# Hybrid decoder trunk: token-major residual, and the down projections as seven products of half matrices with weight sums made by accumulating DMAs

## The chip, the cores and the metric

One NeuronCore of a Trainium2 chip runs the whole program as one launch. The metric is device time in microseconds, the median of the runs; lower is better. TensorE (PE in the profile; PEld is its weight load) multiplies out of SBUF into PSUM, VectorE (DVE) and ScalarE (ACT) do element-wise work, GpSimd (POOL) does small work and issues the DMAs that add, and SyncE (SP) issues the plain DMAs.

## The reference, cut to what matters

Two layers work on x of 512 tokens by 1024 channels in float32; D_FF is 2816.

```python
def swiglu(h, w1, w3, w2):
    return (jax.nn.silu(h @ w1) * (h @ w3)) @ w2
...
    for l in range(DEPTH):
        h = rmsnorm(x, ffn1_norm[l])
        x = x + FFN_RESIDUAL * swiglu(h, ffn1_w1[l], ffn1_w3[l], ffn1_w2[l])
        h = rmsnorm(x, mix_norm[l])
        p = h @ w_in[l]
...
        mix = jnp.concatenate([y_a, y_b, y_c, y_d], axis=-1)
        x = x + mix @ w_out[l]
        h = rmsnorm(x, ffn2_norm[l])
        x = x + FFN_RESIDUAL * swiglu(h, ffn2_w1[l], ffn2_w3[l], ffn2_w2[l])
    return rmsnorm(x, final_norm)
```

The four mixers y_a to y_d (a convolution of 31 taps with a layer norm, a short gated convolution, a pooling and a gating by 128x128 matrices) are the same in both kernels.

## The kernel before, in words

**Products.** Every float32 operand is split into two float32r parts, hi (a ScalarE cast, L92) and lo (a VectorE subtract, L94), and every product is three matmuls (mm3, L97 to L100): hi by hi, hi by lo, lo by hi. PSUM tiles have 512 columns. TensorE takes its work in the order in which the program is written (a manual schedule); the other engines' orders come from the scheduler, and each engine runs its own list in order.

**Residual.** x is held with channels on partitions, as eight tiles x0 to x7 of 128 channels by 512 tokens. The norm is split off: Norm.gained (L144) multiplies a tile by the channel gain while splitting it, which needs no statistic, and the factor 1/rms of each token is applied behind the products. Its statistic comes from squares summed over tiles (L153), four narrow matmuls (rstd_of, L116), a power on GpSimd (L112) and four transposes (spread, L128), all while TensorE is at work on the next stage.

**One feed-forward block** (ffn, L172). For each of 22 tiles of 128 channels of D_FF the up part runs 2 x 8 mm3 of 512 columns, weights stationary and tokens moving, and makes the tile a with sigmoid and three VectorE multiplications (up, L177). The down part (L242) runs for each of 8 channel tiles m of the output 22 mm3, 528 matmuls in all; the sum is scaled by half the norm's factor and added to x[m] (L237), and the next norm takes the tile at once (nxt.add). Four such blocks, f0a, f0b, f1a and f1b, and a mixer stage (mixers, L303) between each layer's two. In the mixers two more pieces matter here: the gating values are products with tokens on the output partitions, 256 columns wide (L362 to L364), and the conformer's 62 taps (L502) run on VectorE beside TensorE's other work.

**Weights.** load_w (L88) loads a tile of up to 128x1024 on SP's queue into one of four raw buffers and splits it into one of four hi and lo pairs, so loads run ahead by as much as these buffers allow. All buffers are named slots: a DMA into a slot waits until the last reader of the earlier tile in it is done.

**Start and end.** Ten matmuls on a constant (WARM) stand first, then the first tile's matmuls follow the loads of x tile by tile (L191 to L216). At the end the last channel tile runs in two halves of the tokens, and class Last (L273) takes each half through the final norm and out.

## Time and profile before

| | |
|---|---|
| median of 3 runs | 1746.85 us (1746.84 to 1747.02) |
| span of the profiled execution | 1744.5 us, 2.35 us under that median |
| PE busy | 1733.9 us, 99% of the span |
| PEld busy | 1438.9 us, 82% |
| DVE busy | 877.9 us, 50% |
| ACT busy | 533.5 us, 31% |
| POOL busy | 22.0 us, 1% |
| DMA | 170.70 MB, mean 98 GB/s |

PE's busy time counts a matmul from its start to its modelled end, and these overlap; the pace is read from the distance between the starts of two matmuls. The profiled execution shows its span, from the first to the last instruction, and the runs give the time of whole executions; a sum made against the span is carried to the runs by their difference.

### The profile page before, as it was taken

How to read it: one execution, taken by the hardware profiler on the slowest of the kernel's cores; microseconds unless marked ns; L12 is line 12 of the kernel's file. 1: busy time of each engine (PE TensorE's matmuls, PEld its weight loads, DVE VectorE, ACT ScalarE, POOL GpSimd, SP SyncE). 2: the span in 40 equal slices, each digit the busy share in tenths (PEclk: the TensorE clock that was granted, in tenths of full speed). 3: DMA queues.
4: the chain of work that ended last, by engine and by line, in shares of the span. 5: the costliest groups of instructions: out<-in, count | busy, mean ns of one | idle time of the engine just before them, and what ended most of it. 6: DMA issues, size and time to landing. Idle time of an engine off the chain costs nothing.

```text
span 1744.5 us, 19177 instructions
## 1 busy us (share of the span) xinstructions
PE 1733.9 (99%) x7882; PEld 1438.9 (82%) x7882; DVE 877.9 (50%) x1145; ACT 533.5 (31%) x693; POOL 22.0 (1%) x22
## 2 busy tenths in 40 slices
PE   9999999999999999999999999999999999999997
PEld 7888888888788888888888888888888888888887
DVE  6444443459864444434344444433697554444333
ACT  5222222233243222222232222222333432222221
POOL 0000000000000000000000000000000000000000
PEclk9999999999999999999999999999999999999999
DMA  5222223332232222333322322233222322223321
GB/s 208 97 97 97 97 88 100 103 115 79 85 103 97 97 97 97 94 95 93 105 97 97 97 97 94 91 100 117 89 85 91 103 97 97 97 97 91 97 91 48
DMA packets 52022, 170.70 MB, mean 98 GB/s; under 512 B 5728, under 2 KB 8928, under 8 KB 51936
## 3 DMA queue, kind: packets, MB, share of 16 engines
q1 hardware_dynamic: 51936, 169.50, 30.0%
q8 instruction: 61, 1.00, 0.2%
q14 instruction: 25, 0.20, 0.0%
HBM read 167.38 MB, written 2.10 MB: 97 GB/s over the span
## 4 chain that ended last, share of the span: by engine, by line
PE 99%; DVE 0%; ACT 0%; DMA 0%; issue 0%; SPq 0%; POOLq 0%; DVEq 0%; ACTq 0%
PE p_f1b L98 7%; PE p_f1b L100 7%; PE p_f1a L98 7%; PE p_f1b L99 7%; PE p_f0b L100 7%; PE p_f0b L99 7%; PE p_f0b L98 7%; PE p_f1a L100 7%; PE p_f1a L99 7%; PE p_f0a L100 7%; PE p_f0a L98 7%; PE p_f0a L99 7%; PE pi_L L98 3%; PE pi_L L99 3%; PE pi_L L100 3%; PE po_L L98 2%
## 5 line engine op out<-in xcount | busy, mean ns | idle before, releaser
L502 DVE SCALAR_TENSOR_TENSOR cg_L<-cv_L,pt,cg_L 128x503 f32<-128x503 f32 (+26 forms) x120 | 83.5, 726 | 2.3 <-ACT cg_L L500 1.8
L98 PE MATMUL p_f1b<-gh_b,whi_f1bb 128*128 128x512 f32 x176 | 68.6, 390 | 0.0
L98 PE MATMUL p_f1a<-gh_a,whi_f1ab 128*128 128x512 f32 x176 | 68.6, 390 | 0.0
L98 PE MATMUL p_f0b<-gh_b,whi_f0bb 128*128 128x512 f32 x176 | 68.6, 390 | 0.0
L98 PE MATMUL p_f0b<-gh_b,whi_f0ba 128*128 128x512 f32 x176 | 68.6, 390 | 0.0
L98 PE MATMUL p_f1a<-gh_a,whi_f1aa 128*128 128x512 f32 x176 | 68.6, 390 | 0.0
L98 PE MATMUL p_f1b<-gh_b,whi_f1ba 128*128 128x512 f32 x176 | 68.6, 390 | 0.0
L100 PE MATMUL p_f0b<-gh_b,wlo_f0bb 128*128 128x512 f32 x176 | 68.5, 389 | 0.0
L100 PE MATMUL p_f1b<-gh_b,wlo_f1bb 128*128 128x512 f32 x176 | 68.5, 389 | 0.0
L100 PE MATMUL p_f0b<-gh_b,wlo_f0ba 128*128 128x512 f32 x176 | 68.5, 389 | 0.0
L100 PE MATMUL p_f1a<-gh_a,wlo_f1ab 128*128 128x512 f32 x176 | 68.5, 389 | 0.0
L100 PE MATMUL p_f1b<-gh_b,wlo_f1ba 128*128 128x512 f32 x176 | 68.5, 389 | 0.0
L99 PE MATMUL p_f1a<-gl_a,whi_f1aa 128*128 128x512 f32 x176 | 68.5, 389 | 0.0
L100 PE MATMUL p_f1a<-gh_a,wlo_f1aa 128*128 128x512 f32 x176 | 68.5, 389 | 0.0
L99 PE MATMUL p_f0b<-gl_b,whi_f0ba 128*128 128x512 f32 x176 | 68.5, 389 | 0.0
L99 PE MATMUL p_f1b<-gl_b,whi_f1ba 128*128 128x512 f32 x176 | 68.5, 389 | 0.0
L99 PE MATMUL p_f1a<-gl_a,whi_f1ab 128*128 128x512 f32 x176 | 68.5, 389 | 0.0
L99 PE MATMUL p_f0b<-gl_b,whi_f0bb 128*128 128x512 f32 x176 | 68.5, 389 | 0.0
L99 PE MATMUL p_f1b<-gl_b,whi_f1bb 128*128 128x512 f32 x176 | 68.5, 389 | 0.0
L98 PE MATMUL p_f0a<-gh_n,whi_f0ab 128*128 128x512 f32 x168 | 65.5, 390 | 0.0
L98 PE MATMUL p_f0a<-gh_n,whi_f0aa 128*128 128x512 f32 x168 | 65.5, 390 | 0.0
L99 PE MATMUL p_f0a<-gl_n,whi_f0aa 128*128 128x512 f32 x168 | 65.4, 389 | 0.0
(1074 smaller groups left out, 4434.7 us busy)
## 6 DMA issues: line engine op xcount, KB each, us to landing
raw_f0ba<-w SPq DMA_DIRECT2D x22, 512.0 KB, 3.7
raw_f0bb<-w SPq DMA_DIRECT2D x22, 512.0 KB, 3.6
raw_f1aa<-w SPq DMA_DIRECT2D x22, 512.0 KB, 3.7
raw_f1ab<-w SPq DMA_DIRECT2D x22, 512.0 KB, 3.6
raw_f1ba<-w SPq DMA_DIRECT2D x22, 512.0 KB, 3.7
raw_f1bb<-w SPq DMA_DIRECT2D x22, 512.0 KB, 3.6
raw_f0aa<-w SPq DMA_DIRECT2D x21, 512.0 KB, 3.7
raw_f0ab<-w SPq DMA_DIRECT2D x21, 512.0 KB, 3.6
```

What stands on the lines that cost most here:

```text
L98: PE.matmul(ps, hi, xh, start=first, stop=False)
L99: PE.matmul(ps, hi, xl, start=False, stop=False)
L100: PE.matmul(ps, lo, xh, start=False, stop=last)
L502: V.scalar_tensor_tensor(acc[:, kk:], v[:, : T - kk], cw, acc[:, kk:], ALU.mult, ALU.add)
```

## The change

The residual and the norms become token-major. x is four tiles x0 to x3 of 128 tokens by 1024 channels. A norm is now whole ahead of the products: per token tile two squares with a sum along the row (Norm.square), the power on GpSimd and one multiplication by factor and gain over 1024 columns (Norm.scale), and then eight TensorE transposes, two casts and two subtracts (Norm.turn) that give the channel-major hi and lo tiles gh0, gh1, gl0 and gl1. Token tiles 2 and 3 come first, tiles 0 and 1 last. The first two tiles of an up part (heads), and the first gate and value in the mixers, therefore run in two halves of 256 columns with a turn of token tiles 0 and 1 between them. silu is one activation out of PSUM.

The down part multiplies the two halves of the tokens, of D_FF and of the output as 2x2 blocks, and takes seven products of halves in place of eight. A product (letters a to g in the names) has 11 channel tiles in six pieces j of two tiles (the last one) and, for each, 2 token tiles x 3 matmuls of 512 columns, activations stationary and weights moving: 66 matmuls, 462 for a block. Sums of activation quarters are made on VectorE (sums), sums of weight quarters by DMAs: gather loads one quarter on SP's queue and then adds another onto it with accum_op on GpSimd's queue. The running weight sum of products b, d and f lies in three tiles tt0, tt1 and tt2, which use the slots of gh0, gh1 and gl0. TensorE's order is a0 b0 a1 b1 to a5 b5, c0 d0 to c5 d5, e0 f0 to e5 f5, then g. Each product's sum is added to one to three places of x straight out of PSUM (add).

The rest: WARM is 40; the gains are loaded as 128x1024 tiles; the weights of w2 and w_out are laid out anew; the output projection has tokens on the output partitions.

```diff
+                S.activation(
+                    sq, xt[b][:, c * T : (c + 1) * T], AF.Square, scale=1.0 / 32.0,
+                    accum_out=self.ss[b][:, c : c + 1],
...
+        def scale(self, b):
...
+                y = rsqrt(v, 1, f"{self.name}{b}")
+                xn = tmp.tile([P, D], F32, tag="xn", name=f"xn_{self.name}{b}")
+                V.scalar_tensor_tensor(xn, xt[b], y, self.gain, ALU.mult, ALU.mult)
...
+        def turn(self, b):
+
+            with tc.high_priority(offset=400):
+                if self.hi is None:
+                    self.hi = [acts.tile([P, 4, T], F32R, tag=f"gh{q}", name=f"gh{q}_{self.name}") for q in range(2)]
+                    self.lo = [acts.tile([P, 4, T], F32R, tag=f"gl{q}", name=f"gl{q}_{self.name}") for q in range(2)]
+                s = slice(b * P, (b + 1) * P)
+                for q in range(2):
+                    ps = bank(f"pt_{self.name}{b}{q}", (P, 4, P))
+                    for k in range(4):
+                        c = (4 * q + k) * P
+                        PE.transpose(ps[:, k], self.xn[b][:, c : c + P], ident)
+                    S.copy(self.hi[q][:, :, s], ps)
+                    V.tensor_tensor(self.lo[q][:, :, s], ps, self.hi[q][:, :, s].bitcast(F32), ALU.subtract)
...
+        for r in (1, 0):
+            for _, _, _, _, ps, w in heads:
+                for e in range(2):
                     for k in range(KD):
                         c = slice(k * P, (k + 1) * P)
-                        mm3(p, w[0][:, c], w[1][:, c], nrm.h[k], nrm.l[k], k == 0, k == KD - 1)
-                    if j == j0 and p is p1:
-                        nrm.stats()
...
-        def down(m, p, c=slice(0, T)):
-            d = tmp.tile([P, T], F32, tag="h1", name=f"d_{name}{m}_{c.start}")
-            V.tensor_tensor(d[:, c], p, half[:, c], ALU.mult)
-            V.tensor_tensor(xt[m][:, c], xt[m][:, c], d[:, c], ALU.add)
-
-        for m in range(KD):
-            parts = ((0, 8), (8, 16), (16, KF))
-            ws = [load_w(w2[f, m, :, a * P : b * P], (b - a) * P, f"{name}c{m}_{a}") for a, b in parts]
...
-            p = psm.tile([P, T], F32, tag="mm", name=f"p2_{name}{m}")
-            for k in range(KF):
-                mm3(p, *weights(k), ah[k], al[k], k == 0, k == KF - 1)
-            down(m, p)
-            nxt.add(m)
...
+                        mm3(
+                            ps[e][:, HALF[r]], w[e][0][:, c], w[e][1][:, c],
+                            nrm.h(k)[:, HALF[r]], nrm.l(k)[:, HALF[r]], k == 0, k == KD - 1,
+                        )
+            if r == 1:
+                turns()
+        for h, j, i, k, ps, _ in heads:
+            out_of(ps[0], ps[1], h, j, i, k)
...
+        tt = [acts.tile([P, 4, T], F32, tag=("gh0", "gh1", "gl0")[q], name=f"tt{q}_{name}") for q in range(3)]
+
+        def tview(j):
+            n = SUB[j][1]
+            return tt[j // 2][:, (j % 2) * 2 : (j % 2) * 2 + n]
...
+        def gather(to, j, one, two):
+
+            k, n = SUB[j]
+            if one is not None:
+                nc.sync.dma_start(to, w2[f, one[0], one[1], :, k : k + n])
+            G.dma_start(to, w2[f, two[0], two[1], :, k : k + n], accum_op=ALU.add)
...
+        def product(banks, j, av, wv, more=False, tiles=(0, 1)):
+            n = SUB[j][1]
+            for t in tiles:
+                ts = slice(t * P, (t + 1) * P)
+                for i in range(n):
+                    mm3(
+                        banks[t], av[0][:, i, ts], av[1][:, i, ts], wv[0][:, i], wv[1][:, i],
+                        not more and j == 0 and i == 0, j == len(SUB) - 1 and i == n - 1, more,
                     )
...
+        def add(r, c, t, ps, sign):
+            b = 2 * r + t
+            xs = xt[b][:, c * T : (c + 1) * T]
+            with tc.high_priority(offset=400):
+                V.scalar_tensor_tensor(xs, ps, 0.5 * sign, xs, ALU.mult, ALU.add)
...
+        for j in J:
+            b11 = piece(0, 0, j, "a")
+            av, wv = asplit(quarter(0, 0, j), j, "a"), wsplit(b11, j, "a")
+            product(X, j, av, wv)
+            gather(tview(j), j, (0, 0), (0, 1))
+            av, wv = asplit(s1[j], j, "b"), wsplit(tview(j), j, "b")
+            product(Z, j, av, wv)
+        for t in range(2):
+            add(0, 0, t, X[t], 1)
+            add(1, 1, t, Z[t], 1)
+        Q = [bank(f"pq{t}_{name}") for t in range(2)]
+        for j in J:
+            t3 = wts.tile([P, SUB[j][1], T], F32, tag="raw", name=f"raw_{name}c{j}", bufs=4)
+            gather(t3, j, (0, 1), (1, 1))
+            av, wv = asplit(quarter(1, 0, j), j, "c"), wsplit(t3, j, "c")
+            product(Q, j, av, wv)
+            gather(tview(j), j, None, (1, 1))
+            av, wv = asplit(s2[j], j, "d"), wsplit(tview(j), j, "d")
+            product(X, j, av, wv, True)
+        for t in range(2):
+            add(1, 1, t, Q[t], -1)
+            add(0, 1, t, X[t], -1)
+            add(1, 0, t, X[t], 1)
+            add(1, 1, t, X[t], -1)
+            nxt.square(2 + t, 1)
+        W = [bank(f"pw{t}_{name}") for t in range(2)]
+        for j in J:
+            b21 = piece(1, 0, j, "e")
+            av, wv = asplit(quarter(0, 1, j), j, "e"), wsplit(b21, j, "e")
+            V.tensor_tensor(s2[j], s2[j], quarter(0, 1, j), ALU.add)
+            product(W, j, av, wv)
+            gather(tview(j), j, None, (1, 0))
+            av, wv = asplit(quarter(1, 1, j), j, "f"), wsplit(tview(j), j, "f")
+            product(Q, j, av, wv, True)
+        for t in range(2):
...
+        for t in range(2):
+            add(0, 0, t, W[t], 1)
+            nxt.square(t, 0)
+        held = []
+        for j in J:
+            b22 = piece(1, 1, j, "g")
+            av, wv = asplit(s2[j], j, "g"), wsplit(b22, j, "g")
+            if j < 4:
+                product(Z, j, av, wv, True)
+            else:
+                held.append((j, av, wv))
+            if j == 3 and not end:
+                for t in range(2):
+                    nxt.turn(2 + t)
+        for t in range(2):
+            for j, av, wv in held:
+                product(Z, j, av, wv, True, (t,))
+            add(0, 1, t, Z[t], 1)
+            nxt.square(t, 1)
+            if end:
+                nxt.last(t)
+            else:
+                nxt.scale(t)
```

The orders show where this puts the instructions. On SP's queue, around the start of f0a's down part, this stands before (raw_f0ac: the weights of the first two output tiles):

```order
L90 DMA raw_f0ab21_1730<-w13 128x1024
L90 DMA raw_f0ac0_0_1794<-w2 128x1024
L90 DMA raw_f0ac0_8_1800<-w2 128x1024
L90 DMA raw_f0ac0_16_1806<-w2 128x768
L90 DMA raw_f0ac1_0_1888<-w2 128x1024
```

and this stands there now (raw_f0aa2 to 4: product a; tt: the first quarter of product b's sums, in two calls each; raw_f0ac: product c):

```order
L91 DMA raw_f0aa2_1908<-w2 128x1024
L91 DMA raw_f0aa3_1952<-w2 128x1024
L91 DMA raw_f0aa4_1996<-w2 128x1024
L253 DMA tt2_f0a_1815<-w2 128x1024
L253 DMA tt0_f0a_1813<-w2 128x1024 x2
L253 DMA tt1_f0a_1814<-w2 128x1024 x2
L253 DMA tt2_f0a_1815<-w2 128x512
L91 DMA raw_f0aa5_2040<-w2 128x512
```

The loads into tt stand behind five loads of product a, and tt2 (piece 4) stands ahead of tt0 (pieces 0 and 1). On GpSimd's queue, which held nothing for a down part before, the adding DMAs now stand in the same order:

```order
L254 DMA tt2_f0a_1815<-w2 128x1024
L254 DMA tt0_f0a_1813<-w2 128x1024 x2
L254 DMA tt1_f0a_1814<-w2 128x1024 x2
L254 DMA tt2_f0a_1815<-w2 128x512
L254 DMA tt0_f0a_1813<-w2 128x1024 x2
```

The last of these rows is already product d's addition. On VectorE, between products d and e, f of f0a, eight additions to x (L281) now stand between the splits of e0 and of f0 (before, a down tile had one multiplication and one addition, between other tiles' splits):

```order
L99 TENSOR_TENSOR wlo_f0ae0_2354<-raw_f0ae0_2346,whi_f0ae0_2352 128x1024
L264 TENSOR_TENSOR al_f0af1_2416<-a11_f0a_224,ah_f0af1_2414 128x512
L281 SCALAR_TENSOR_TENSOR x2_83<-pq0_f0a_2076,x2_83 128x512
L281 SCALAR_TENSOR_TENSOR x3_84<-pq1_f0a_2077,x3_84 128x512
L281 SCALAR_TENSOR_TENSOR x0_81<-px0_f0a_1818,x0_81 128x512
L281 SCALAR_TENSOR_TENSOR x2_83<-px0_f0a_1818,x2_83 128x512
L281 SCALAR_TENSOR_TENSOR x1_82<-px1_f0a_1819,x1_82 128x512
L281 SCALAR_TENSOR_TENSOR x2_83<-px0_f0a_1818,x2_83 128x512
L281 SCALAR_TENSOR_TENSOR x3_84<-px1_f0a_1819,x3_84 128x512 x2
L99 TENSOR_TENSOR wlo_f0af0_2376<-tt0_f0a_1813,whi_f0af0_2374 128x1024
```

The split of f0's weights thus follows all additions. On VectorE at the end of the first mixer stage, where the next block's operands are made, this stood before (x: the output's addition, gl: the gained lo part, ready tile by tile):

```order
L547 TENSOR_TENSOR x0_84<-po_L00_3361,x0_84 128x512
L547 TENSOR_TENSOR x1_85<-po_L01_3374,x1_85 128x512
L150 SCALAR_TENSOR_TENSOR gl_b0_0_3549<-x0_84,pt_108,gh_b0_0_3547 128x512
L150 SCALAR_TENSOR_TENSOR gl_b0_1_3562<-x1_85,pt_108,gh_b0_1_3560 128x512
L157 TENSOR_TENSOR sq_b0_1_3564<-sq_b0_0_3551,sq_b0_1_3564 128x512
```

and this now (nv: the mean square, xn: a normalized token tile, gl0: its lo part behind the transposes):

```order
L145 SCALAR_TENSOR_TENSOR xn_b03_3914<-x3_84,ry_b03_3912,gain2_3883 128x1024
L640 TENSOR_TENSOR x0_81<-po_L001_3826,x0_81 128x512
L640 TENSOR_TENSOR x1_82<-po_L010_3703,x1_82 128x512
L142 TENSOR_SCALAR nv_b00_3935<-ss_b00_3923 128x1
L640 TENSOR_TENSOR x1_82<-po_L011_3845,x1_82 128x512
L145 SCALAR_TENSOR_TENSOR xn_b00_3939<-x0_81,ry_b00_3937,gain2_3883 128x1024
L142 TENSOR_SCALAR nv_b01_3960<-ss_b01_3948 128x1
L161 TENSOR_TENSOR gl0_b0_3968<-pt_b020_3970,gh0_b0_3966 128x4x128
L145 SCALAR_TENSOR_TENSOR xn_b01_3964<-x1_82,ry_b01_3962,gain2_3883 128x1024
L161 TENSOR_TENSOR gl0_b0_3968<-pt_b030_3984,gh0_b0_3966 128x4x128
```

The lo part of token tile 3, which the next block's second matmul reads, now stands behind the norms of all four token tiles.

## Rows read from the trace of the kernel before

**Rows 1.** The page: busy time, granted clock, and the chain by engine.

```profile
PE 1733.9 (99%) x7882; PEld 1438.9 (82%) x7882; DVE 877.9 (50%) x1145; ACT 533.5 (31%) x693; POOL 22.0 (1%) x22
PEclk9999999999999999999999999999999999999999
PE 99%; DVE 0%; ACT 0%; DMA 0%; issue 0%; SPq 0%; POOLq 0%; DVEq 0%; ACTq 0%
```

**Rows 2.** Waits of PE, the longest of four: us in total, times, longest us.

```profile
PE pst_a L120 <- ACT sq_a L279: 1.4, 1, 1.4
```

**Rows 3.** Timeline of PE, a down part: start us, us; 19 steps apart.

```profile
299.62 0.39 PE L99 MATMUL p_f0a<-a_f0a9l,whi_f0ac 128*128 128x512 f32 x1
...
303.93 0.39 PE L100 MATMUL p_f0a<-a_f0a15h,wlo_f0ac 128*128 128x512 f32 x1
```

**Rows 4.** Timeline of PE, the gating values of 256 columns; 41 steps apart.

```profile
397.72 0.28 PE L362 MATMUL pgv_L<-whi_L0g,gh_m 128*128 128x256 f32 x1
...
402.64 0.28 PE L364 MATMUL pgv_L<-whi_L0g,gl_m 128*128 128x256 f32 x1
```

**Rows 5.** The chain that ended last: start us, us, what.

```profile
24.09 0.79 PE pst_n L120 x8
...
30.49 0.44 PE pr_n L131 x4
...
472.55 1.72 PE pmn_L L509 x4
```

**Rows 6.** Timeline of the start; the last row begins steady work.

```profile
1.12 4.64 PE L199 MATMUL pd<-mean_w 128*128 128x128 f32 x20 [1.12 <-DVE expo L85]
...
18.47 0.39 PE L98 MATMUL p_f0a<-gh_n,whi_f0aa 128*128 128x512 f32 x1
```

**Rows 7.** Groups of DVE and ACT by line and form: count, busy us, mean ns.

```profile
L94 DVE TENSOR_TENSOR wlo_f0ba<-raw_f0ba,whi_f0ba 128x1024 fp32r<-128x1024 f32 x22 | 26.9, 1224 | 7.5 <-ACT whi_f0ba L92 7.5
...
L92 ACT CAST whi_f0ba<-raw_f0ba 128x1024 fp32r<-128x1024 f32 x22 | 23.2, 1052 | 74.5 <-issue 64.1 <-PE p_f0b L99 9.3 <-PE po_L L99 1.1
...
L183 DVE TENSOR_TENSOR a_f1b<-p_f1b,a_f1b 128x512 f32<-128x512 f32 x22 | 15.1, 690 | 53.8 <-PE p_f1b L100 53.8
...
L150 DVE SCALAR_TENSOR_TENSOR gl_m<-x,pt,gh_m 128x512 fp32r<-128x512 f32 x16 | 11.9, 744 | 0.0
...
L155 ACT ACTIVATE sq_m<-x 128x512 f32<-128x512 f32 x16 | 9.8, 615 | 0.0
```

**Rows 8.** Timeline of ACT: a copy of 512 columns out of PSUM.

```profile
532.96 0.58 ACT L136 COPY R_b<-pr_b 128x512 f32<-128x512 f32 x1
```

**Rows 9.** Groups of POOL: the powers.

```profile
L112 POOL TENSOR_TENSOR ry_gl_L<-bva_L,expo 128x2 f32<-128x2 f32 x4 | 4.4, 1109 | 61.4 <-DVE bva_L L374 61.4
...
L112 POOL TENSOR_TENSOR ry_a<-rv_a,expo 128x2 f32<-128x2 f32 x2 | 1.4, 696 | 345.1 <-DVE rv_a L125 345.1
```

**Rows 10.** DMA issues: KB each, median us from issue to landing.

```profile
raw_f0ba<-w SPq DMA_DIRECT2D x22, 512.0 KB, 3.7
...
out<-o SPq DMA_DIRECT2D x8, 256.0 KB, 2.3
```

**Rows 11.** Windows at the start: last two columns are DMA share and GB/s.

```profile
4.00:6.00 2.00, 2.00 (x10) 1.93 (x9) 1.07 (x2) 1.28 (x2) 0.00 (x0) 1.00 0.88 301
...
14.00:16.00 2.00, 1.90 (x9) 1.23 (x8) 2.00 (x4) 2.00 (x4) 0.00 (x0) 1.00 1.04 414
```

**Rows 12.** Timeline of SP: two issues one behind the other.

```profile
9.55 0.33 SPq L90 DMA_DIRECT2D raw_f0ab<-w  x1
...
10.28 0.33 SPq L90 DMA_DIRECT2D raw_f0aa<-w  x1
```

**Rows 13.** Timeline in the first mixer stage: the last taps, and the matmul that reads them.

```profile
466.68 1.97 DVE L502 SCALAR_TENSOR_TENSOR cg_L<-cv_L,pt,cg_L 128x483 f32<-128x483 f32 x3
...
472.39 1.88 PE L509 MATMUL pmn_L<-cg_L,mean_w 128*128 128x512 f32 x4
```

**Rows 14.** The chain in the last microseconds: the last matmul of the last product.

```profile
1733.83 0.13 PE p_f1b L100
```

More of the change, by code (lines that the diff above doesn't have):

```diff
@@ L22 @@
 KF = DFF // P
+KH = KF // 2
 DEPTH = 2
@@ L48, in trunk @@
 @with_exitstack
-def trunk(ctx: ExitStack, tc: tile.TileContext, x, par, tab, w13, w2, wi, wg, wo, woa, out):
+def trunk(ctx: ExitStack, tc: tile.TileContext, x, par, gains, tab, w13, w2, wi, wg, wo, out):
     nc = tc.nc
@@ L110, in rsqrt, with mm3 @@
+    def mm3(ps, sh, sl, mh, ml, first, last, more=False):
+        PE.matmul(ps, sh, mh, start=first, stop=False, skip_group_check=more)
+        PE.matmul(ps, sh, ml, start=False, stop=False, skip_group_check=more)
+        PE.matmul(ps, sl, mh, start=False, stop=last, skip_group_check=more)
     def rsqrt(v, n, name):
@@ L304, in mixers @@
+    def mixers(l, nrm, nxt, turns):
         base = l * C_LAYER
         nm = f"L{l}"
-        slot[0] = 0
+        scratch = Scratch(nm)
         def col(c):
@@ L551, in trunk @@
[L551 to L561 removed]
+        wa = []
@@ new lines, in mixers @@
+        for b in (2, 3):
+            nxt.turn(b)
+    ctx.enter_context(tc.manual_schedule(engines={mybir.EngineType.PE}))
+    pd = bank("pd")
+    for i in range(WARM):
+        PE.matmul(pd[:, 0:P], mean_w, mean_w, start=True, stop=True)
+    nrm = Norm("n0", 0)
+    for b in (2, 3):
+        for c in range(2):
+            nrm.square(b, c)
+        nrm.scale(b)
+    for b in (0, 1):
+        nc.sync.dma_start(xt[b], x[b])
+    for b in (0, 1):
+        for c in range(2):
+            nrm.square(b, c)
+        nrm.scale(b)
@@ new lines, in trunk, with turns @@
+    pt = const.tile([P, C_ALL], F32, name="pt")
+    nc.sync.dma_start(pt, par)
+    for b in (2, 3):
+        nrm.turn(b)
+    for l in range(DEPTH):
+        def turns(nrm=nrm):
+            for b in (0, 1):
+                nrm.turn(b)
+        nx = Norm(f"m{l}", 3 * l + 1)
+        ffn(2 * l, nrm, nx, f"f{l}a", turns)
+        nrm = nx
+        def turns(nrm=nrm):
+            for b in (0, 1):
+                nrm.turn(b)
+        nx = Norm(f"b{l}", 3 * l + 2)
+        mixers(l, nrm, nx, turns)
+        nrm = nx
+        def turns(nrm=nrm):
+            for b in (0, 1):
+                nrm.turn(b)
+        nx = Norm(f"a{l + 1}", 3 * l + 3)
+        ffn(2 * l + 1, nrm, nx, f"f{l}b", turns, end=l + 1 == DEPTH)
```

546 lines of the change are left out of this document (253 added, 293 removed).

## The prediction

> **What bounds the kernel now.** The page comes first. PE is busy for 99% of the span, its granted clock is full in every slice, and the chain that ended last lies on PE for 99% [rows 1]. The view of waits then shows that PE hardly waits: four waits, the longest 1.4 us [rows 2]. So the time is TensorE's instruction count times its pace, and the timeline gives the pace: 19 matmuls of 512 columns start within 4.31 us, 0.2268 us each [rows 3], and 41 of 256 columns within 4.92 us, 0.120 us each [rows 4], so a half costs slightly more than half. In the chain, a float32 pass of 512 columns takes 1.72 / 4 = 0.43 us, or 0.1075 us per 128 columns; a transpose takes 0.11 us, a narrow statistic matmul about 0.2 us (eight, in pairs, 0.79 us per four) [rows 5].
>
> **Matmuls removed and added.** The two orders, counted: 512-column matmuls go from 7334 to 6656 (-678 x 0.2268 = -153.8 us), 256-column ones from 324 to 1152 (+828 x 0.120 = +99.4), transposes from 36 to 200 (+164 x 0.11 = +18.0), narrow ones from 48 to 16 (-32 x 0.2 = -6.3). Sum: **-42.8 us**. In parts: a down part has 462 matmuls of 512 columns in place of 528, which for four is -59.9; the halves at the starts of stages cost +6.3, the last tile's halves that go give back 0.9. If TensorE never waited more than now, the span would be 1744.5 - 42.8. The rest asks where it now has to.
>
> **Start of the program: +8 (4 to 10).** Now 20 passes of the constant take 4.64 us, 0.232 us each, which is half pace against 0.1075, and steady work begins at 18.47 us [rows 6], with 48 matmuls (10.9 us of the counted work) done by then: 7.6 us are lost. Afterwards no product can start before x2 and x3, the gains, and their whole norm. WARM of 40 is 80 passes: 1.12 + 4.64 + 60 x 0.1075 = 12.2 us. Then follow transposes, a copy of 512 columns (0.58 us [rows 8]) and the weight's split (1.05 for the cast, 1.22 for the subtract [rows 7]) behind the copies on their engines: the second matmul stands at about 17.4 us, less 1.9 us of counted work, 15.5 lost in place of 7.6. Below: the data alone, 3.24 MB at 301 to 414 GB/s [rows 11], would let it begin at some 13 us; above, if all 80 passes go at 0.232, at 20 us or later.
>
> **Turns inside a stage: +8.7 (6 to 15).** Six times (two norms' heads in each layer, and the mixers' first products) TensorE transposes token tiles 0 and 1 and then needs their hi and lo parts. The transposes take 16 x 0.11 = 1.76 us; three of the four copies, 0.58 us each, and the subtracts behind them (0.69 us for 512 columns out of PSUM [rows 7]) end about 3.2 us after the start of the turn. TensorE waits about 1.45 us (1.0 to 2.5) each time.
>
> **End of the mixers to the next block, twice: +11.2 (9 to 13).** The operands of the next products now wait for a norm instead of being gained tile by tile. On VectorE gl of tile 3 stands behind the additions, mean squares and multiplications of all four token tiles. From the start of the last output matmuls TensorE has about 12.7 us of work. VectorE's chain is additions of 0.69, a power of 0.7 to 1.1 us on GpSimd [rows 9], four multiplications over 1024 columns at about 1.35 us (between 1.22 for a subtract and 2 x 0.744 for the same form on 512 [rows 7]) and a turn's copy and subtract: its end comes 17.3 to 19.3 us from that start. Difference 4.6 to 6.6; I take 5.6.
>
> **From products c, d to e, f, four times: +9.6 (2 to 10).** VectorE has eight additions at 0.69 us (one operand from PSUM) before the split of f0's weights (1.22): about 5.5 us before the second matmul of f0 can go with all before it done, while e0 gives TensorE 12 x 0.2268 = 2.7 us and its queue little more. 2.4 us each time (0.5 if the scheduler's queue runs ahead, 2.6 if not). After a, b and after e, f there are four additions, which e's or c's first matmuls cover.
>
> **The first weight sum of each down part: +26 (18 to 33).** This is the term on which the answer rests. The tiles tt take the slots of gh0, gh1 and gl0, which the last up products read until about 0.6 to 2.9 us before the up part's end (the last use of gl0 ends first). So none of the quarters can be loaded early, as the weights of product a can. tt2 (piece 4) stands first on SP's queue; one issue takes 0.7 us with its wait [rows 12]; tt0's load is issued about 2.2 us before the up part's end and lands 3.7 us later [rows 10], 1.5 us into the down part. Only then can GpSimd issue the addition onto it, behind the same for tt2. The trace holds no adding DMA. Below, one that costs what a plain load does lands at 1.5 + 3.7 = 5.2 us; above, one that costs two loads in a row at 8.9 us. Then the cast (1.05) and the subtract (1.22) follow. TensorE has only a0, 2.7 us of matmuls, since b0 stands second in its order: it waits 4.6 to 8.3 us for the second matmul of b0. I take 6.5, the middle, four times. What is queued behind: on ScalarE the cast of b0 stands ahead of a1's, so product a can't step in. Later pieces have their loads issued by then and are one pair of products (5.4 us) apart.
> The Trainium skill ("Collectives: The Full Stack", section "The bandwidth ceiling: the fold count and why AG ≠ RS ≠ AR") says of collective transfers that an adding one moves at half the rate of a copy, because it has two sources to read. No run here shows it for a load into SBUF. By it the landing would be at the upper end, and this term +33.
>
> **The end: -2 (-3 to 0).** Now the last matmul ends at 1733.96 of 1744.5 us [rows 14]: 10.5 us follow, 0.8 of it counted as work above. Afterwards an addition (0.69), a square (0.615), a power (0.7 to 1.1), a multiplication (1.4) and a store of 512 KB, between 2.3 us (256 KB) and 3.7 [rows 10], follow: 7.5 to 8 us with the hand-overs.
>
> **Costed at nothing.** In a down part (104.8 us of TensorE) VectorE has about 87 us of splits, sums and additions and ScalarE about 64: covered while each runs ahead; without that cover the excess would be a few us at the joints costed above. The loads, 14.4 MB, and additions, 11.5 MB, are 65 us at 400 GB/s. The conformer's taps now run beside a mixer stage in which VectorE also has more norms; before, the last tap ended 468.64, 3.7 us before the matmul that reads them [rows 13], and products cover the same now; if that margin goes, some 3 us twice.
>
> **The sum.** -42.8 + 8 + 8.7 + 11.2 + 9.6 + 26 - 2 = about +19 us: a span of 1763.5. The median before lies 2.35 us above its profiled span, so the same for the new one gives **1766 us** (1749 to 1780 with the terms' ranges taken together).
>
> **Rivals.** *Faster: the first weight sums are there in time.* If the load of tt0 lands well before the up part ends (its slot free early, as gh0's last reads may be scheduled before the last tile), b0 waits for nothing and the sum is -6.6: 1740 us. For it speaks that the DMA queues are idle for most of an up part; against it that the slots are read by every up product up to the last, and that b0 has one product's cover only. Halving the wait at b0 to 3.2 us would still be +6; it decides at about 1.6 us (no change) and is outside the noise on the fast side below 0.8 us. 0.30.
>
> *The clock falls.* In the trace of before a clock drop isn't to be seen, but neither is a wait above 1.4 us [rows 1, 2]; what it does show is that after idleness 20 passes at the start run at half pace for 4.64 us [rows 6]. If each of six long waits (four at b0, two at the mixers' end) is followed by such a stretch, each loses 2.3 us more: +14, 1780 us. The half pace is 1.2 GHz in place of 2.4. The Trainium skill ("TensorE: Matmul & The Clock Gate", section "Part 1: The HAM clock gate") holds that an engine which has idled is clocked at half until it has been busy again; the start of this trace agrees (0.232 against 0.1075 us a pass), the middle has no wait to show it. 0.15.
>
> *The adding DMAs bound the down parts.* With loads of 36 us (14.4 MB at 400 GB/s) and additions of 28.8 us times their cost k against a load's, the transfers need 114 us (TensorE's work with its waits) at k = 2.7; at 3 about 8 us more a block, +32: 1800 us; at 4, 37 us a block: 1915. Nothing in the trace prices k; at 2 they are hidden but for the first. 0.13.
>
> That the products aren't fewer can be put aside: the order has 462 per down part.
>
> **How the numbers follow.** Waits eat the gain, as summed: 0.42; faster 0.30; clock 0.15; transfers 0.13. 0.2% (3.5 us) is about what a measurement of this kernel can tell from no change. The forecast's own range touches 1749, so a small part of it (0.06) lies within 0.2%, and of the fast case a tenth does: faster 0.27, same 0.09, slower 0.64. The range reaches from 1734 (the fast case with its other terms at their low ends) to 1798, short of the transfer-bound case.
>
> **What would show it.** Right: PE waits of some 5 to 8 us at pz (product b) in all four blocks, ended by the split of tt0 and behind it the adding DMA; 2 to 3 us at product f's first matmul, ended by VectorE; waits of 1 to 2 us at turns and of about 5 at gl in the blocks after the mixers; steady work from about 17 us; some 0.227 us a matmul between waits. The clock rival shows as slices below 9 in the granted clock where the down parts begin, the transfer rival as PE waits spread over all pieces of c, d, e, f with the DMA share near 1. It is wrong if the waits at b0 are below 1 us, or if they come back at every piece.

## The result, and the profile after

The changed kernel takes 1802.28 us (median; 1800.57 to 1803.4) against 1746.84 us of the kernel before: a ratio of 1.0316, 95% interval 1.0302 to 1.0331. It is 3.2% slower, above the range of the prediction. The direction was the forecast one; the size is almost three times as large (55.4 us for 19).

The page of the changed kernel (the first part's engines, the granted clock and the DMA share in 40 slices, and the chain by engine), to be read against [rows 1]:

```profile
PE 1717.4 (95%) x8192; PEld 1438.7 (80%) x8192; DVE 929.5 (52%) x1177; ACT 630.7 (35%) x886; POOL 115.9 (6%) x138
...
PEclk9999998999999999989999999899999999999899
DMA  5322239743322222379433323695433132232982
...
PE 90%; DVE 6%; DMA 2%; ACT 1%; issue 1%; POOL 0%; POOLq 0%; ACTq 0%; DVEq 0%
```

PE's share has fallen from 99% to 95%. The granted clock is below full in four slices, and these are the slices in which a down part's wait lies; there and in the slice behind each, the DMA row reaches 6 to 9. The view of PE's waits (total, times, longest) names the place; four waits of at most 1.4 us stood there before [rows 2]:

```profile
PE pz_f1a L107 <- ACT whi_f1ab L97: 11.6, 1, 11.6
PE pz_f0b L107 <- ACT whi_f0bb L97: 10.9, 1, 10.9
PE pz_f1b L107 <- ACT whi_f1bb L97: 10.5, 1, 10.5
PE pz_f0a L107 <- ACT whi_f0ab L97: 10.5, 1, 10.5
PE p_f0b L108 <- DVE gl_b L161: 2.9, 2, 2.3
...
PE pq_f1a L108 <- DVE wlo_f1af L99: 1.5, 1, 1.5
```

All four long waits are at the first matmul of product b, for the cast of its first weight sum; the mixers' ends (gl_b) and f's first piece follow far behind. The timeline of PE at f0a's shows what each costs:

```profile
266.78 0.39 PE L109 MATMUL px_f0a<-whi_f0aa,al_f0aa 128*128 128x512 f32 x1
277.70 0.80 PE L107 MATMUL pz_f0a<-whi_f0ab,ah_f0ab 128*128 128x512 f32 x1 [10.53 <-ACT whi_f0ab L97]
278.96 0.80 PE L108 MATMUL pz_f0a<-wlo_f0ab,ah_f0ab 128*128 128x512 f32 x1 [0.46 <-DVE wlo_f0ab L99]
279.56 0.63 PE L109 MATMUL pz_f0a<-whi_f0ab,al_f0ab 128*128 128x512 f32 x1
279.98 0.63 PE L107 MATMUL pz_f0a<-whi_f0ab,ah_f0ab 128*128 128x512 f32 x1
...
282.87 0.40 PE L107 MATMUL px_f0a<-whi_f0aa,ah_f0aa 128*128 128x512 f32 x1
```

From the end of a0's work (266.78 + 0.23) to the first matmul of a1 (282.87) lie 15.9 us, of which b0's twelve matmuls at 0.2268 are 2.7: 13.1 us lost, and 13.7, 15.2 and 13.7 in the other blocks by the same reading, some 55.8 in all. After the wait the matmuls start 0.42 us apart, then 0.23 again. The windows (last three columns: granted clock, DMA share, GB/s) show two things:

```profile
264.00:266.00 2.00, 2.00 (x10) 1.65 (x10) 1.37 (x3) 0.00 (x0) 0.00 (x0) 1.00 1.00 406
...
272.00:274.00 2.00, 0.00 (x0) 0.00 (x0) 0.00 (x0) 0.00 (x0) 0.88 (x1) 0.50 1.05 205
...
280.00:282.00 2.00, 2.00 (x7) 1.57 (x6) 1.81 (x3) 1.15 (x2) 0.33 (x2) 0.57 1.05 207
282.00:284.00 2.00, 2.00 (x10) 1.64 (x9) 1.10 (x2) 1.16 (x2) 0.63 (x1) 1.00 1.04 205
```

The clock goes to 0.50 (1.2 of 2.4 GHz) while PE is idle and is back at 282. And the DMA engines are full from 264 on: at 406 GB/s while loads are on their way, at 205 to 207 once the additions are.

The same place in the timeline of the queues and of the cast (start, us, and what it waited for):

```profile
261.54 4.23 SPq L253 DMA_DIRECT2D tt_f0a<-w  x6
...
266.01 1.04 POOL L254 DMA_DIRECT2D tt_f0a<-w  x1 [253.06 <-DVE s_f0a L189]
...
267.21 1.87 POOL L254 DMA_DIRECT2D tt_f0a<-w  x2 [0.17 <-PE px_f0a L109]
...
276.61 1.04 ACT L97 CAST whi_f0ab<-tt_f0a 128x1024 fp32r<-128x1024 f32 x1 [9.01 <-DMA tt_f0a<-w]
...
279.15 1.04 ACT L97 CAST whi_f0ab<-tt_f0a 128x1024 fp32r<-128x1024 f32 x1 [0.56 <-DMA tt_f0a<-w]
```

All six loads of the first sums are issued within 4.2 us, and the addition onto piece 0 at 267.2, 2.9 us into the down part (its load's landing had been put at 1.5). But the sum is there only at 276.6, 9.4 us after its issue, and the next piece's 2.5 us behind it. The issues (KB each, median us to landing) agree:

```profile
tt_f0a<-w POOLq DMA_DIRECT2D x15, 512.0 KB, 11.3
...
tt_f0a<-w SPq DMA_DIRECT2D x5, 512.0 KB, 4.7
raw_f0ac<-w SPq DMA_DIRECT2D x5, 512.0 KB, 8.0
...
raw_f0ag<-w SPq DMA_DIRECT2D x5, 512.0 KB, 3.5
```

An addition lands after 11.3 us, and product c's plain loads, issued among additions, after 8.0, while product g's, with none about, take 3.5 (3.7 before [rows 10]).

**The sum, term by term** (us; lost time is the distance between starts of PE's matmuls less their count times the pace of [rows 3, 4]):

| term | predicted | measured |
|---|---|---|
| matmuls removed and added | -42.8 | -42.8 (by count; the pace is unchanged) |
| start of the program | +8 | +9.7 (17.3 us lost for 7.6) |
| six turns | +8.7 | +8.5 (1.41 each) |
| mixers to the next block, twice | +11.2 | +13.1 |
| products c, d to e, f, four times | +9.6 | +7.1 |
| first weight sum, four times | +26 | +55.8 |
| the end | -2 | +1 |
| not listed: ScalarE's last split of the mixers, twice | | +2 |
| sum | +19 | +54.4, against 55.8 between the two spans |

### The profile page after: what moved, and what is told of

Its sections match the earlier page's. It is cut to its first block, busy times and chain, and to the rows that moved or that the text cites. A ratio compares the mean times of both kernels' runs of the same rounds, so it can differ in the third digit from the quotient of the medians.

```text
span 1800.3 us, 20605 instructions
## 1 busy us (share of the span) xinstructions
PE 1717.4 (95%) x8192; PEld 1438.7 (80%) x8192; DVE 929.5 (52%) x1177; ACT 630.7 (35%) x886; POOL 115.9 (6%) x138
## 3 DMA queue, kind: packets, MB, share of 16 engines
q1 hardware_dynamic: 52704, 184.67, 30.7%
q0 software_dynamic: 13824, 46.14, 13.1%
## 4 chain that ended last, share of the span: by engine, by line
PE 90%; DVE 6%; DMA 2%; ACT 1%; issue 1%; POOL 0%; POOLq 0%; ACTq 0%; DVEq 0%
PE p_f1b L108 5%; PE p_f0b L108 5%; PE p_f0a L109 5%; PE p_f1b L109 4%; PE p_f1b L107 4%; PE p_f0b L109 4%; PE p_f0a L108 4%; PE p_f0a L107 4%; PE p_f0b L107 4%; PE p_f1a L108 4%; PE p_f1a L109 4%; PE p_f1a L107 4%; PE pi_L L108 2%; PE pi_L L109 2%; PE pi_L L107 2%; PE po_L L107 1%
## 5 line engine op out<-in xcount | busy, mean ns | idle before, releaser
L587 DVE SCALAR_TENSOR_TENSOR cg_L<-cv_L,pt,cg_L 128x507 f32<-128x507 f32 (+26 forms) x120 | 83.0, 731 | 0.7
L108 PE MATMUL p_f1b<-gl_b,whi_f1ba 128*128 128x512 f32 (+1 forms) x192 | 72.6, 378 | 2.9 <-DVE gl_b L161 2.9
L108 PE MATMUL p_f0b<-gl_b,whi_f0ba 128*128 128x512 f32 (+1 forms) x192 | 72.2, 376 | 2.9 <-DVE gl_b L161 2.9
L107 PE MATMUL p_f1b<-gh_b,whi_f1ba 128*128 128x512 f32 (+1 forms) x192 | 72.4, 377 | 2.1 <-ACT gh_b L160 2.1
L107 PE MATMUL p_f0b<-gh_b,whi_f0ba 128*128 128x512 f32 (+1 forms) x192 | 72.3, 376 | 2.1 <-ACT gh_b L160 2.1
L107 PE MATMUL p_f0a<-gh_n,whi_f0aa 128*128 128x512 f32 (+1 forms) x192 | 72.1, 375 | 2.1 <-ACT whi_f0aa L97 1.8
L109 PE MATMUL p_f0a<-gh_n,wlo_f0aa 128*128 128x512 f32 (+1 forms) x192 | 72.1, 376 | 1.9 <-DVE wlo_f0aa L99 1.9
L108 PE MATMUL p_f0a<-gl_n,whi_f0aa 128*128 128x512 f32 (+1 forms) x192 | 72.0, 375 | 1.4 <-DVE gl_n L161 1.4
L109 PE MATMUL p_f1b<-gh_b,wlo_f1ba 128*128 128x512 f32 (+1 forms) x192 | 72.3, 377 | 0.0
L109 PE MATMUL p_f0b<-gh_b,wlo_f0ba 128*128 128x512 f32 (+1 forms) x192 | 71.9, 375 | 0.0
```

The lines of the kernel that those rows point to most:

```text
L107: PE.matmul(ps, sh, mh, start=first, stop=False, skip_group_check=more)
L108: PE.matmul(ps, sh, ml, start=False, stop=False, skip_group_check=more)
L109: PE.matmul(ps, sl, mh, start=False, stop=last, skip_group_check=more)
L587: V.scalar_tensor_tensor(acc[:, kk:], v[:, : T - kk], cw, acc[:, kk:], ALU.mult, ALU.add)
```

## Experiments

Two theories stood at the start. **Batch**: the wait at b0 is that of one batch; six loads and six additions go at once and share the DMA engines, so their first result is late, and only TensorE's order makes it felt. **Latency**: an adding DMA is slow by itself, some 9 us, whatever runs beside it. A third came out of the first run. **Transfers**: additions move at half rate, so that up to the last of product d the transfers are as long as TensorE's work, and the loss is not tied to b0.

A measure for all runs is the length of a down part, from the start of its first product matmul to that of its last. For the changed kernel's f0a these two rows of PE's timeline give it, 385.51 - 264.29 = 121.2 us:

```profile
264.29 0.39 PE L107 MATMUL px_f0a<-whi_f0aa,ah_f0aa 128*128 128x512 f32 x1
...
385.51 0.39 PE L109 MATMUL pz_f0a<-whi_f0ag,al_f0ag 128*128 128x512 f32 x1
```

461 steps of 0.2268 are 104.6 us, plus 1.8 of transposes in all blocks but the last. The same two rows of each run:

| kernel | median us | f0a | f0b | f1a | f1b |
|---|---|---|---|---|---|
| changed | 1802.28 | 121.2 | 121.8 | 123.5 | 120.0 |
| a as a whole, then b | 1803.88 | 123.2 | 120.7 | 124.0 | 119.9 |
| ... and c's additions left out | 1752.98 | 110.7 | 109.4 | 110.6 | 108.1 |
| b's additions left out | 1754.78 | 111.7 | 109.8 | 109.9 | 108.3 |
| slots swapped | 1799.85 | 119.9 | 121.3 | 121.6 | 119.5 |
| e moved ahead of b | 1760.55 | 112.5 | 110.5 | 112.3 | 109.2 |
| eight plain products | 1798.83 | 121.2 | 121.2 | 121.2 | 119.5 |
| norm order | 1784.85 | 120.1 | 119.3 | 120.1 | 117.6 |
| kept busy, 128 columns | 1806.92 | 123.0 | 122.6 | 122.9 | 122.6 |
| kept busy, 512 columns | 1799.04 | 120.4 | 120.0 | 122.5 | 120.4 |
| e up and norm order | 1748.95 | 111.3 | 109.3 | 111.2 | 107.9 |
| ... and turns covered | 1739.23 | 111.8 | 109.1 | 110.9 | 107.5 |

**1. Product a as a whole, then b.** Only the order of the code, and so of TensorE, is changed:

```diff
             product(X, j, av, wv)
             gather(tview(j), j, (0, 0), (0, 1))
+        for j in J:
             av, wv = asplit(s1[j], j, "b"), wsplit(tview(j), j, "b")
             product(Z, j, av, wv)
```

> TensorE does all six pieces of product a before the first of product b, nothing else is changed. Batch theory (the first weight sum lands about 12 us after the down part begins, because six loads and six adding DMAs share the DMA engines): product a gives 15 us of cover, so the wait of 10.5 to 11.6 us at b0, its second half of 0.5 us and the stretch at half pace behind it all go, 13 to 15 us in each of four blocks: 1746 to 1752 us. Rival, the adding DMAs bound the whole down part: the wait comes back at later pieces of b, c or d, and the time stays above 1785 us.

1803.88 us, ratio 1.0323 (1.0305 to 1.034): nothing gained. The batch theory falls as it was put. The wait at b0 has gone; three to five short ones stand inside b, and in each block a long one at the last piece but one of product c, whose weight sum now lands late. PE's waits, the cast that this piece waits for, and the windows there:

```profile
PE pq_f1b L107 <- ACT whi_f1bc L97: 4.5, 1, 4.5
...
PE pz_f0a L108 <- DVE wlo_f0ab L99: 3.2, 5, 0.8
```

```profile
328.29 1.04 ACT L97 CAST whi_f0ac<-raw_f0ac 128x1024 fp32r<-128x1024 f32 x1 [9.60 <-DMA raw_f0ac<-w]
```

```profile
310.00:320.00 10.00, 9.62 (x42) 7.48 (x41) 9.14 (x12) 6.13 (x9) 2.59 (x3) 1.00 1.06 244
320.00:330.00 10.00, 5.58 (x23) 4.05 (x22) 2.48 (x4) 1.71 (x3) 0.86 (x1) 0.91 1.07 235
```

TensorE waits with the DMA engines full (1.06 to 1.07). The down part is as long as in the changed kernel: the loss was moved, which points to a shortage of transfer, not to one late result.

**2. The additions for b left out.** Product b multiplies by the loaded quarters alone:

```diff
-            gather(tview(j), j, (0, 0), (0, 1))
+            k, n = SUB[j]
+            nc.sync.dma_start(tview(j), w2[f, 0, 0, :, k : k + n])
```

> The adding DMAs of product b's weight sums are left out (b multiplies by the loaded quarters alone; the adds of c, d and f remain). If the adds make the wait: the loads land about 5 us after the slots are free, the wait at b0 falls from about 11 us to 1 to 2 us, TensorE keeps its clock, and the time falls by 4 x 10 to 13 us, to 1750 to 1762 us. If it is the late slot and the loads: the wait stays above 5 us and the time above 1778 us.

1754.78 us (one execution), 47.5 less: the wait at b0 is at most 0.8 us for the cast and 0.8 for the subtract, the down parts 108 to 112 us. The additions make the loss; the late slots alone do not.

**3. Slots swapped.** Piece 0 is loaded and added first:

```diff
-        tt = [acts.tile([P, 4, T], F32, tag=("gh0", "gh1", "gl0")[q], name=f"tt{q}_{name}") for q in range(3)]
+        tt = [acts.tile([P, 4, T], F32, tag=("gl0", "gh0", "gh1")[q], name=f"tt{q}_{name}") for q in range(3)]
```

> The three tiles of sums take the slots gl0, gh0, gh1 in place of gh0, gh1, gl0, so that piece 0 is the first to be loaded and added. Batch theory: piece 0's addition is issued 1.5 us sooner and runs ahead of the other five, so it has the DMA engines to itself for a while: the wait at b0 falls by 2 to 5 us in each block, 1782 to 1794 us. Rival, an adding DMA has a long latency of its own (9 us or so) whatever runs beside it: only the earlier issue counts, 1 to 1.5 us a block, 1796 to 1798 us.

1799.85 us, ratio 1.0304 (1.0289 to 1.0319), which overlaps the changed kernel's interval: less than either theory said. The wait at b0 did fall, by 2.6 to 3.0 us, and PE's waits show where a part of it went:

```profile
PE pz_f0a L107 <- ACT whi_f0ab L97: 7.9, 1, 7.9
...
PE pq_f0b L108 <- DVE wlo_f0bf L99: 2.3, 1, 2.3
```

The losses at product f's start are 1.8, 4.1, 4.2 and 3.9 us (1.8 each before the swap). Of the 2 us and more that three blocks lose there anew, 0.5 to 0.8 are a longer wait for VectorE, and the rest is half pace: the granted clock, which stays at 1.00 there in the changed kernel, is 0.50 for 3.4 us behind this wait. The longer wait goes back to the transfers: product c's last sum lands no sooner than before the swap, and in f0b VectorE works without a gap from its split to f0's. So a gain at b0 is paid at f in part, and this run alone doesn't tell how much of that is transfer.

**4. Transfers by themselves.** A small program in place of the kernel, with the tiles' sizes and queues of the down part:

```python
for i in range(4):
    G.dma_start(alone, quarter(4 + i, i), accum_op=ALU.add)
...
    for j in range(5):
        G.dma_start(six[j], quarter(12 + r, j), accum_op=ALU.add)
```

> A small program that leaves out the whole computation and only moves data: four plain loads of 512 KB one behind the other, four adding DMAs one behind the other, twice six loads together and then six adding DMAs together, one adding DMA beside five loads. Batch theory: an adding DMA alone lands in 4 to 6 us, six together in 11 to 16 us for the last, at about half of the loads' GB/s. Rival (latency): one alone takes 9 us or more, and six together hardly more than that.

Its DMA issues (count, KB each, median us to landing) and queues (packets, MB, share of the 16 engines):

```profile
q0 software_dynamic: 2448, 8.91, 36.8%
q1 hardware_dynamic: 4176, 15.21, 32.0%
...
six<-w SPq DMA_DIRECT2D x12, 512.0 KB, 5.9
six<-w POOLq DMA_DIRECT2D x12, 512.0 KB, 10.7
mixed<-w SPq DMA_DIRECT2D x5, 512.0 KB, 6.2
...
alone<-w SPq DMA_DIRECT2D x4, 512.0 KB, 3.6
alone<-w POOLq DMA_DIRECT2D x4, 512.0 KB, 5.7
mixed<-w POOLq DMA_DIRECT2D x1, 512.0 KB, 9.3
```

Latency is out: an addition alone lands in 5.7 us, a load in 3.6. Together they hold one another up: six additions have a median of 10.7, and one addition beside five loads takes 9.3. Its windows of six additions and of six loads:

```profile
72.00:76.00 4.00, 0.00 (x0) 0.00 (x0) 1.00 1.06 210
...
54.00:58.00 4.00, 1.99 (x4) 0.00 (x0) 1.00 1.02 412
```

210 GB/s for 412. Per byte the adding queue held the engines (36.8 / 8.91) / (32.0 / 15.21) = 1.96 times as long. The Trainium skill ("Collectives: The Full Stack", section "The bandwidth ceiling: the fold count and why AG ≠ RS ≠ AR") gives a collective's addition half a copy's rate because it reads two sources; the 1.96 agrees in the rate, for additions onto tiles in SBUF; what the engines read is not in the trace. In the changed kernel itself, where loads and additions run side by side, the same ratio is (13.1 / 46.14) / (30.7 / 184.67) = 1.71.

**What the transfers theory says in numbers.** A product's weights are 2.88 MB. In the changed kernel's f0a the first load of a sum is issued at 261.5 and the last sum of product c lands at 329.1, 67.6 us later, and the engines are full in between (the last two columns are the DMA share and GB/s):

```profile
262.00:329.00 67.00, 56.00 (x239) 45.54 (x238) 42.89 (x54) 30.02 (x40) 20.94 (x24) 0.92 1.05 255
```

They move 9.98 MB of additions in this time (b's, c's and d's, 8.65 MB, and the first of f's, which stand ahead of c's last one in the queue) and 7.08 MB of loads (b's and c's, 5.77, the last of a's and the first of e's): 48 us at 210 GB/s and 17 at 412, 65 us. TensorE's work on a to d is 264 x 0.2268 = 59.9 us, and 2.7 us of it, with a cast and a subtract of 0.6 and 0.7, must follow that last sum. By this estimate a to d can't be done in less than 69 us from the down part's start, 9 more than their matmuls; it took 73, and c's last sum lay ready for some 4 us of it before TensorE came to it. The stretch from the first load to c's last sum hardly depends on the order: it is 68 to 70 us in the four blocks of the changed kernel, 66 to 69 with a as a whole ahead of b, 68 with the slots swapped, and 56 to 57 with b's additions left out. The next runs test this.

**5. Product e moved ahead of b.** It needs no sum, and gives 15 us of work for 7 us of loads. TensorE's order becomes a0 e0 to a5 e5, b, c0 d0 to c5 d5, f, g:

```diff
+            b21 = piece(1, 0, j, "e")
+            av, wv = asplit(quarter(0, 1, j), j, "e"), wsplit(b21, j, "e")
+            product(W, j, av, wv)
+        for t in range(2):
+            add(0, 0, t, X[t], 1)
+            add(0, 0, t, W[t], 1)
+        for j in J:
             av, wv = asplit(s1[j], j, "b"), wsplit(tview(j), j, "b")
             product(Z, j, av, wv)
```

> TensorE's order in a down part is a0 e0 a1 e1 to a5 e5, then b, then c0 d0 to c5 d5, then f, then g: product e, which needs no sum of weights, is done ahead of b. Transport theory (adding DMAs move about 205 GB/s, half of a load's rate; from the up part's end to the last of d the transfers of a, b, c and d take some 62 us, as long as TensorE's work on them, so about 13 us are lost in whatever order these four stand): with 15 us more of other work ahead of the sums, the loss at b0 goes and 0 to 4 us a block come back at c, d or f: 1750 to 1764 us. Rival (it is the first sum's delay and the queue order alone, and other sums stall as they did with a ahead of b): the loss moves to c or f and the time stays above 1785 us.

1760.55 us, ratio 1.0082 (1.0067 to 1.0097): 41.7 us less than the changed kernel with the same instructions. No wait in a down part is above 1.7 us, and the clock stays. The windows of f0a's down part:

```profile
262.00:285.00 23.00, 23.00 (x103) 19.05 (x102) 13.28 (x17) 9.23 (x12) 4.50 (x5) 1.00 0.96 277
285.00:300.00 15.00, 13.98 (x62) 11.27 (x61) 9.93 (x14) 10.36 (x15) 3.56 (x5) 1.00 1.06 327
300.00:315.00 15.00, 14.83 (x65) 11.93 (x64) 10.38 (x13) 4.37 (x8) 7.41 (x9) 1.00 1.06 222
```

The DMA engines are as full as before, but PE (first number behind the length) is busy beside them.

**6. Product a as a whole, then b, and c's additions left out.**

```diff
-            gather(t3, j, (0, 1), (1, 1))
+            k, n = SUB[j]
+            nc.sync.dma_start(t3, w2[f, 0, 1, :, k : k + n])
```

> Product a as a whole ahead of b, as in the first experiment, and the adding DMAs of product c's sums are left out (c multiplies by the loaded quarters alone). Transport theory: 2.88 MB of additions, 14 us of transfer, are gone ahead of the wait at c, so this wait (4.5 us, with the half pace behind it) and most waits inside b and d go: 1748 to 1758 us. Rival (the order of casts and subtracts on ScalarE and VectorE holds c back): the waits and 1800 us stay.

1752.98 us (one execution), 50.9 less than the first experiment. Taking away 2.88 MB of additions frees about the same, 10 to 14 us a block, whether they are b's (run 2, at the place of the wait) or c's (here, behind it). Together with run 1, where TensorE waits while the engines are full, this shows the resource: the DMA engines' time up to c's last sum. Holding f's additions back until c's are done, which might free some of it, was not tried.

**7. Eight plain products**, in the token-major layout: no sums, no adding DMA, each weight quarter loaded and split twice.

```diff
+        plain(1, 0)
+        plain(1, 1)
+        plain(0, 0)
+        plain(0, 1, (1,))
```

> The token-major layout with eight plain products of halves in the down parts (528 matmuls, no sums of activations or weights, no adding DMA; rows of tokens 2 and 3 first, then 0 and 1; each weight quarter is loaded and split twice). This is the layout's price alone. From the measured terms: the changed kernel less its loss at b0 (56 us) and at f0 (7 us), plus 264 matmuls of 0.2268 us (60 us): 1797 to 1803 us, that is 52 us above before. If the layout costs little and the products are what went wrong in more places than the waits show: below 1785 us.

1798.83 us, ratio 1.0297 (1.0282 to 1.0313). So the layout alone costs 52 us, as the terms said, and its down parts take 121.2 us, as long as the changed kernel's, which have 66 matmuls fewer: what the seven products save, their transfers took back.

**8. Norm order.** Three small things:

```diff
-WARM = 40
+WARM = 20
...
-            nxt.scale(b)
+            nxt.scale(b, 400 if b >= 2 else -400)
...
-            add(0, 1, t, X[t], -1)
-            add(1, 0, t, X[t], 1)
-            add(1, 1, t, X[t], -1)
-            nxt.square(2 + t, 1)
...
+            if j == 1:
+                rest()
```

> Three small things in the changed kernel at once, at places apart: WARM 20 in place of 40; the norms of token tiles 0 and 1 at the start and at the mixers' ends with a low priority, so that VectorE takes one of the two behind the lo parts of tiles 2 and 3; and of the eight additions between products d and e, f only the two of c's sum ahead of f0, the other six behind piece 1. If the terms are as read from the profile: the start gets 2 to 3 us shorter, the waits at the two mixers' ends 1.3 us each, the waits of 1.5 us at f0 go in all four blocks: 1788 to 1794 us. The wait at b0 stays as it is. Rival (these waits are covers for one another): less than 4 us.

1784.85 us, ratio 1.0222 (1.0205 to 1.0239): 17.4 less, above what was expected. f0's four waits are gone (7 us), and steady work starts 3.2 us sooner, of which 2.0 are left at the first down part. The mixers' ends gave 3 and 4 us, not 1.3: the second wait there fell from 2.3 to 0.8 us, and the clock, which had cost 1.5 us at the first end and 2.4 at the second, no longer fell. The windows behind the first, in the changed kernel and here:

```profile
534.00:544.00 10.00, 7.40 (x47) 7.20 (x48) 4.00 (x7) 1.23 (x3) 0.55 (x1) 0.83 0.17 55
```

```profile
531.00:541.00 10.00, 9.11 (x73) 8.91 (x74) 3.82 (x7) 1.06 (x3) 0.55 (x1) 1.00 0.17 54
```

**9 and 10. The two together, and with the turns covered.** The tenth run sets the transposes of token tiles 0 and 1 one group of 24 half matmuls earlier:

```diff
+                    if r == 1 and h == e == 1:
+                        turns()
...
-            if r == 1:
-                turns()
```

> Product e ahead of b, and the three small things of the last run together (WARM 20, norms of token tiles 0 and 1 at low priority, six of the eight additions behind piece 1 of f). If the terms are independent, as read from the profiles: 1760.5 less 3 (start), 6 (the mixers' ends with the half pace behind them) and 6.5 (f0): 1744 to 1747 us, no different from the kernel before within the measurement. Rival (product f's first sums are held up by the transfers and not by the additions on VectorE, so that the wait at f0 stays): 1750 to 1753 us.

> The same, and the transposes of token tiles 0 and 1 stand one group of 24 half matmuls (2.9 us) earlier in TensorE's order, in all six turns, so that copies and subtracts (1.45 us beyond the transposes) run beside it. 1.4 us less in each of six places than the run beside it: 1736 to 1739 us, 0.4 to 0.6 % faster than the kernel before. Rival (the transposes then wait for the norm of tiles 0 and 1 instead): no gain over the run beside it.

1748.95 us, ratio 1.0016 (1.0007 to 1.0025), and 1739.23 us, ratio 0.9957 (0.9943 to 0.997). The second is faster than both kernels, than the one before by 0.4%. The turns gave 9.7 us for 8.4. The ninth is 2 us above its expectation: f's wait went, but the down parts are still 3 to 5 us longer than their matmuls and transposes. Some 2 us of this stand at b, and what holds TensorE there is VectorE: the four additions to x that came ahead of b together with product e stand in front of the subtract of b's second piece, whose cast had ended at 291.5. In f0a:

```profile
291.84 1.28 DVE L281 SCALAR_TENSOR_TENSOR x<-px_f0a,x 128x512 f32<-128x512 f32 x2
293.04 1.28 DVE L281 SCALAR_TENSOR_TENSOR x<-pw_f0a,x 128x512 f32<-128x512 f32 x2
...
295.50 0.50 PE L108 MATMUL pz_f0a<-wlo_f0ab,ah_f0ab 128*128 128x512 f32 x1 [1.11 <-DVE wlo_f0ab L99]
```

The rest stands at c and d, where casts still wait for sums. Moving those four additions was not tried.

**11 and 12. TensorE kept busy in the wait.** Unused matmuls between a0 and b0, 40 on a constant of 128 columns, then 44 copies of a0's first of 512:

```diff
+            if j == 0:
+                pk = bank(f"pk_{name}")
+                for _ in range(44):
+                    PE.matmul(pk, av[0][:, 0, 0:P], wv[0][:, 0], start=True, stop=True)
```

> The changed kernel with 40 matmuls on a constant (80 passes of 128 columns, 8.6 us at full pace) put between a0 and b0 in each down part, into a bank of their own. They fill most of the wait at b0 and compute nothing that is used. If the clock's fall in the wait costs time behind it (b0's matmuls start 0.43 us apart in place of 0.227 until they are nearly done): the granted clock stays 1.00 and each block is 2 us shorter, 1792 to 1796 us. If the half pace is paid for by the later sums (transfers bound the whole stretch to product d): the time stays within 2 us of 1802.

> As the run before, with 44 matmuls of 512 columns (copies of a0's first, 10.0 us at full pace, into a bank of their own, unused) in place of the 128-column ones, since the clock fell behind those too. If the clock now stays and its fall was a cost of its own: b0 ends 2 us sooner in each block, 1792 to 1796 us. If the transfers up to product d bound the stretch anyway (as the swapped slots suggested: 2.7 us less at b0, 2.3 us more at f0): the time stays within 3 us of 1802 although the granted clock stays at 1.00.

1806.92 us, ratio 1.0344 (1.033 to 1.0358), and 1799.04 us, ratio 1.0296 (1.0279 to 1.0313), which overlaps the changed kernel's interval. In the eleventh the clock fell all the same, later, and the time is 4.6 us above the changed kernel's, which neither branch had; the cause is open. In the twelfth it stayed at 1.00 in f0a and f0b, and fell in f1a and f1b. Its windows at b0 in f0a and in f1b:

```profile
280.00:284.00 4.00, 3.29 (x14) 2.72 (x15) 3.81 (x4) 3.45 (x6) 1.36 (x2) 1.00 1.07 213
```

```profile
1682.00:1686.00 4.00, 3.14 (x7) 2.34 (x8) 3.75 (x4) 3.46 (x5) 0.86 (x1) 0.65 1.07 211
```

Where it stayed, the down parts are 0.8 and 1.7 us shorter than the changed kernel's; where it fell, 1.0 shorter and 0.4 longer. So the half pace at b0 is worth at most 1 to 2 us a block beside the transfers; two blocks of each kind don't settle it closer.

## Why the prediction was wrong

**The step that failed** is "The first weight sum of each down part: +26 (18 to 33)". Place, engine, chain and count were right, and so was the price of one addition: 5.7 us alone lies between its bounds of one load and two loads in a row. What was wrong is that the term was made of durations of single transfers. The bound of "one that costs two loads in a row" held for an addition with the DMA engines to itself; here five more loads and five more additions were on them, and it took 9.4 us. The sentence that the later pieces "have their loads issued by then and are one pair of products (5.4 us) apart" saw their queues and not their share of the same 16 engines. Measured: 10.5 to 11.6 us of wait to the first matmul, 0.5 to the second, and 2 to 3 us of half pace, 13 to 15 in place of 6.5. That is 29.8 of the 36.3 us between forecast and result. The same slip stands in what was costed at nothing: loads and additions of a down part were put at 400 GB/s alike, 65 us; at the measured 412 and 210 they are 90.

**The rival of the transfers** had the right cause and the wrong account. It set all loads and additions of a block against all of TensorE's time, and found them hidden at k = 2. k is 1.96 for additions by themselves and 1.71 in the changed kernel. But three of the four products that need sums stand in the first four of seven, and no quarter of a sum can be fetched before the up part is all but over, so the account had to be made up to c's last sum: 68 to 70 us of full DMA engines, beside 59.9 us of TensorE's work on a to d.

**The rival of the clock** came true beside the forecast, at all four waits and at the mixers' ends. At the mixers' ends it cost 1.5 and 2.4 us, the part of that term that was not foreseen. The page "TensorE: Matmul & The Clock Gate" of the Trainium skill (section "Part 1: The HAM clock gate") holds that an engine that has idled is clocked at half until it has been busy again; the matmuls 0.42 us apart behind all four waits agree.

**The rival on the fast side** did not hold: the first sums were 10 us late. Its sum without the wait is -7.3 by the terms, not -6.6, on which nothing hangs.

**Right** were the matmul counts and pace, the turns (8.5 for 8.7), the mixers' ends less the clock (9.2 for 11.2), the joint of c, d and e, f (7.1 for 9.6) and VectorE's and ScalarE's work costed at nothing. Smaller misses: the start is 1.7 us longer than put, and the end 3 us (the last store lands 2.6 us after its issue, as put, but the span ends another 2.6 us behind that, where it was 0.9 before; the profile doesn't show why). Not listed was ScalarE's split of the last mixer operand ahead of the output projection, 1 us each.

## What to carry to other kernels

Before DMAs are given work (sums, extra loads), add up their engine time against the compute engine's up to each point at which something must have landed, not over a whole stage, and take no single transfer's latency for that of one in a batch. When such an account doesn't close, hiding the first wait only moves it (run 1); work that needs none of the transfers, set ahead of them, closes it (run 5), and a layout's small waits, taken one by one, were worth 17 and 10 us here (runs 8 and 10), a part of the first because the clock then stayed up. Work that is moved takes its followers along: product e's and a's additions to x became the next wait (run 9).
